# RMS norms on TensorE: row sums by four 128x32 column tiles, the spread by two tiles of 64 rows

## The chip, the cores and the metric

The kernel runs on one core of a Trainium2 chip. The metric is the device time of one launch, in microseconds. The kernel before takes 2510.49 us, the median of three runs (2510.39 to 2510.75). A core has five engines that work side by side, each through its own list of instructions in order: TensorE (PE, with its weight loads shown as PEld), VectorE (DVE), ScalarE (ACT), GpSimd (POOL) and SyncE (SP, which issues transfers). They wait for each other through semaphores.

## The reference

The reference is one inference step of a streaming encoder with two layers of width 1024, for 640 tokens (512 of a new stream, 8 x 16 of running ones). A layer is a half-step SwiGLU feed-forward block (inner width 2816), a mixer (short convolution and banded attention with 8 heads, gated and merged), and another half-step feed-forward block. Each starts with an RMS norm, and a last norm follows the second layer. All is float32.

```python
def _rmsnorm(x, g):
    xf = x.astype(jnp.float32)
    y = xf * lax.rsqrt(jnp.mean(xf * xf, axis=-1, keepdims=True) + EPS)
    return y.astype(x.dtype) * g

for l in range(DEPTH):
    x = x + 0.5 * _swiglu(_rmsnorm(x, norm_ffn1[l]), w_ffn1_gu[l], w_ffn1_down[l])
    m = _mixer(_rmsnorm(x, norm_mix[l]), ...)
    x = x + m
    x = x + 0.5 * _swiglu(_rmsnorm(x, norm_ffn2[l]), w_ffn2_gu[l], w_ffn2_down[l])
y = _rmsnorm(x, norm_final)
```

So there are seven norms: `a0`, the mixer's `m0`, `b0`, `a1`, `m1`, `b1`, and the final one.

## The kernel before

The state x lies transposed in the core's SBUF: eight tiles `x[k]` of 128 partitions (features) by 640 columns (tokens). Weights come as a stream of 128x1024 slabs (`raw`, issued by SP), are split by ACT and DVE into a high and a low part (`whi`, `wlo`, lines 320 and 325), and each product of float32 matrices is made of three matmuls in a fast format: high by high, high by low, low by high. Results gather in PSUM, whose tiles of one bank are named `att` or `pr`, and of two banks `acc`. Products that are computed by Strassen-like combinations of halves (line 410) write 128x320 at a time; the plain ones (line 387) write the two halves of 320 tokens in turn.

A norm's factor, one number a token, is applied after the product that needs it, so the product needn't wait for it. Its making has these steps:

1. ACT squares the eight tiles, DVE adds them into one 128x640 tile (`ssum`; in the mixer a part of `ya`).
2. `Stats.sums` (line 487): TensorE adds over the partitions. For each of five blocks of 128 tokens the block of `ssum` is the stationary operand and a column of ones the moving one, and the result, 128 tokens on 128 partitions, is one column of a PSUM tile (`nps`). Plain float32 is used here, for which the trace shows two records of weight load and matmul for each instruction.
3. `roots`, or `root` and `diagonal` (lines 599 and 603): ACT takes the square root of five columns, DVE the reciprocal.
4. `Stats.turn` (line 497): DVE multiplies the identity by each of the five columns: a 128x640 tile of five diagonals, written over `ssum`.
5. the spread (lines 609 and 469): TensorE multiplies a 128x128 tile of ones with the diagonals, in two matmuls of 320 tokens. It has each token's factor on all partitions (`nbc`), which ACT copies to SBUF (`rho` or `rr`).

The order of PE's instructions is written out by hand everywhere; in the feed-forward blocks' ends, in the mixer's second half and in the final norm the orders of DVE and ACT are too, while in the attention and between, a planner orders DVE's and ACT's steps. Products stand between steps 2 and 5 on PE, so that the root and the diagonal are made beside them: one part of a product of `gate_up` in a1, b0 and b1, more in a0 (`opening`) and in the mixers (line 1405, the values' product, with 128x512 at a time).

The final norm (`Final.all`) works on two parts of the tokens, 384 and 256. The last down product (line 1711) makes the first part for all eight `m`, then the second. The first part's sums (line 1680, six matmuls, for two tiles of squares) and spread (line 1740) stand within the second part's products. The second part's sums (line 1725) are added up piece by piece as the squares come; only the last piece, root, diagonal, spread and the eight outputs (line 1744, DVE, each followed by a transfer out) come after the last product.

For comparison, the sample attention uses column tiles of 32 already (lines 1546 and 1579: four heads' pairs beside each other, written to four ranges of 32 partitions), and the scores of the prompt attention use tiles of 64 rows (line 1452: two heads beside each other, written to two banks).

Of the kernel before, what the change touches and what calls it, by code (L numbers as in the profile page):

```python
# [10 lines left out]
F32 = mybir.dt.float32  # L11
F32R = mybir.dt.float32r
AF = mybir.ActivationFunctionType
ALU = mybir.AluOpType
PSUM = bass.MemoryType.PSUM

P = 128
D = 1024
L = 2
SEQ = 512  # L20
# [3 lines left out]
HT = T // 2  # L24
# [5 lines left out]
FF = 2816  # L30
KT = D // P
FT = FF // P
FH = FT // 2
CT = CW // P
CHUNK = 64
# [5 lines left out]
NP = KT // 2  # L41
NT = T // P

# [3 lines left out]

PARTS = slice(0, 3 * P), slice(3 * P, T)

# [14 lines left out]
O_G1, O_GM, O_G2, O_GF = 0, L * KT, 2 * L * KT, 3 * L * KT  # L64
# [44 lines left out]
def mixer_order():  # L109
# [74 lines left out]
def halves(t):  # L184
    return t.rearrange("p (a b) -> p a b", a=2)
# [3 lines left out]
def trunk(ctx: ExitStack, tc: tile.TileContext, xin, wst, small, pbias, samplebias, kcache, vcache,  # L189
          yout, ko, vo, co):  # L190
    nc = tc.nc
    PE, DVE, ACT, POOL, SP = nc.tensor, nc.vector, nc.scalar, nc.gpsimd, nc.sync

    cp = ctx.enter_context(tc.tile_pool(name="cp", bufs=1))
# [6 lines left out]
    ps = ExitStack()  # L201
# [31 lines left out]
    slabs, n = [], 0  # L233
# [10 lines left out]
    for kind, units in stages():  # L244
        n = sum(2 if z in ("gu", "mix") else 1 for z in units)
# [115 lines left out]
    class Tiles:  # L361


        def __init__(self):
            self.cur = None
            self.at = self.n = 0
# [47 lines left out]
    sm = cp.tile([P, NSM], F32, name="sm")  # L414
# [3 lines left out]
    ident = cp.tile([P, P], F32, name="ident")  # L418
    make_identity(nc, ident)
    ones = cp.tile([P, P], F32, name="ones")  # L420
    POOL.memset(ones, 1.0)
    epst = cp.tile([P, 1], F32, name="epst")
    POOL.memset(epst, EPS)
    early = cp.tile([P, 1], F32, name="early")
# [4 lines left out]
    x = [xp.tile([P, T], F32, name=f"x{k}") for k in range(KT)]  # L429
    for k in range(KT):  # L430
# [4 lines left out]
        if k % 2 == 0:  # L435
            c = slice(k * P, (k + 2) * P)
            SP.dma_start(raws[0][:, c], wst[0][:, c])

    def norm(name, goff, ssum, keep):

        out = []
        for k in range(KT):
            g = sm[:, goff + k : goff + k + 1]
            hi = hp.tile([P, T], F32R, tag="hhi", name=f"hhi{name}_{k}")
            lo = hp.tile([P, T], F32R, tag="hlo", name=f"hlo{name}_{k}")
            ACT.activation(hi, x[k], AF.Copy, scale=g)
            DVE.scalar_tensor_tensor(out=lo, in0=x[k], scalar=g, in1=hi.bitcast(F32),
                                     op0=ALU.mult, op1=ALU.subtract)
            out.append((hi, lo))
        for k in range(KT):  # L450
            if k == 0:
                ACT.activation(ssum, x[k], AF.Square)
            else:
                sq = tmp(f"sq{name}_{k}")
                ACT.activation(sq, x[k], AF.Square)
                DVE.tensor_tensor(out=ssum, in0=ssum, in1=sq, op=ALU.add)
        st = Stats(name)
        st.caps, st.rr = (keep.tile([P, T], F32, name=f"{n}{name}") for n in ("caps", "rr"))

        def sums():  # L460
            st.sums([ssum], st.bank)
            st.roots()
            st.turn(ssum, st.r)

        def spread():
            for a in range(2):
                c = slice(a * HT, (a + 1) * HT)
                ps = pr(f"nbc{name}_{a}")[:, :HT]
                PE.matmul(ps, ones, ssum[:, c], start=True, stop=True)
                ACT.copy(st.rr[:, c], ps)  # L470

        return out, st, (sums, spread)

    class Stats:


        def __init__(self, name):
            self.name = name
            self.s = sp.tile([P, NT], F32, tag="nrms", name=f"nrms{name}", bufs=3)
            self.r = sp.tile([P, NT], F32, tag="ninv", name=f"ninv{name}", bufs=2)  # L480

        def sums(self, parts, ps):

            self.ps = ps
            for c in range(NT):
                for i, z in enumerate(parts):
                    PE.matmul(ps[:, c : c + 1], z[:, c * P : (c + 1) * P], ones[:, 0:1],
                              start=i == 0, stop=i == len(parts) - 1)

        def roots(self):  # L490
            ACT.activation(self.s, self.ps[:, :NT], AF.Sqrt, bias=epst[:, 0:1], scale=1.0 / D)
            DVE.reciprocal(self.r, self.s)

        def turn(self, out, r):

            n = out.shape[1] // P
            DVE.tensor_tensor(out=out.rearrange("p (c t) -> p c t", c=n),
                              in0=ident.unsqueeze(1).to_broadcast([P, n, P]),
                              in1=r.unsqueeze(2).to_broadcast([P, n, P]), op=ALU.mult)

    def scaled(out, ps, rr):
        DVE.tensor_tensor(out=halves(out), in0=two(ps), in1=halves(rr), op=ALU.mult)
# [1 line left out]
    class Expand(Stats):  # L504
# [93 lines left out]
        def root(self):  # L598
            ACT.activation(self.s, self.ps[:, :NT], AF.Sqrt, bias=epst[:, 0:1], scale=1.0 / D)

# [3 lines left out]
            self.turn(self.ssum, self.r)  # L604

        def spread(self, ps):
            for a in range(2):
                c = slice(a * HT, (a + 1) * HT)
                PE.matmul(ps[a], ones, self.ssum[:, c], start=True, stop=True)
            for a in range(2):  # L610
                ACT.copy(self.rho[:, a * HT : (a + 1) * HT], ps[a])

            ACT.activation(early, epst, AF.Silu)
            self.known = True
# [1041 lines left out]
    class Final:  # L1656
# [7 lines left out]
        def all(self, ops):  # L1664
            ws = [[tiles.take() for _ in ops] for m in range(KT)]
            flush()
            rr = pool[0].tile([P, T], F32, tag="cap", name="frr", bufs=5)[:, PARTS[0]]
            A, B = PARTS

            for m in range(KT):  # L1670
                self.product(0, m, ops, ws[m])
                self.take(0, m, m < KT - 1)
            ends = self.ssum[0], self.sq
            for m in range(KT):
                self.product(1, m, ops, ws[m])
                if m == 1:
                    self.ps = att("npsf0")[:, : A.stop // P]
                    for b in range(A.stop // P):
                        for i, z in enumerate(ends):
                            PE.matmul(self.ps[:, b : b + 1], z[:, b * P : (b + 1) * P], ones[:, 0:1],  # L1680
                                      start=i == 0, stop=i == 1)
                    self.root(0)
                if m == 4:
                    ACT.copy(rr, self.spread(0))
                if m == 5:
                    self.ps = acc("npsf1")[:, :, 0]
                    self.add(self.ssum[1], True)
                if m > 4:
                    self.add(self.sq)
                self.take(1, m, m < 4)  # L1690
                if m == 2:
                    self.turn(0)
                for k in {5: (0,), 6: (1, 2)}.get(m, ()):
                    self.out(k, A, rr)
            self.add(self.sq, False, True)
            self.root(1)
            for k in range(3, 6):
                self.out(k, A, rr)
            self.turn(1)
            for k in range(6, KT):  # L1700
                self.out(k, A, rr)
            ps = self.spread(1)
            for k in range(KT):
                self.out(k, B, ps)

# [16 lines left out]
        def add(self, z, start=False, stop=False):  # L1722

            for b in range(2):
                PE.matmul(self.ps[:, b : b + 1], z[:, b * P : (b + 1) * P], ones[:, 0:1],
                          start=start, stop=stop)

        def root(self, a):
            cs = slice(PARTS[a].start // P, PARTS[a].stop // P)
            ACT.activation(self.st.s[:, cs], self.ps, AF.Sqrt,  # L1730
                           bias=epst[:, 0:1], scale=1.0 / D)

# [2 lines left out]
            DVE.reciprocal(self.st.r[:, cs], self.st.s[:, cs])  # L1735
            self.st.turn(self.ssum[a], self.st.r[:, cs])

        def spread(self, a):
            ps = att(f"nbcf{a}")[:, : PARTS[a].stop - PARTS[a].start]
            PE.matmul(ps, ones, self.ssum[a], start=True, stop=True)  # L1740
            return ps

        def out(self, k, c, rr):
            DVE.scalar_tensor_tensor(out=x[k][:, c], in0=x[k][:, c], scalar=sm[:, O_GF + k : O_GF + k + 1],
                                     in1=rr, op0=ALU.mult, op1=ALU.mult)
            (ACT if c == PARTS[1] and k % 2 else SP).dma_start(yout[:, k, c], x[k][:, c])

# [93 lines left out]
def _layout(inputs):  # L1841
    i = {n: np.asarray(a) for n, a in inputs.items()}
    tok = np.concatenate([i["x_prompt"].reshape(SEQ, D), i["x_sample"].reshape(NB * TS, D)])
    xin = tok.T.reshape(KT, P, T).transpose(1, 0, 2)
# [61 lines left out]
```

## Time and profile before

| | |
|---|---|
| median of three runs | 2510.49 us |
| span of the profiled execution, first to last instruction | 2509.0 us |
| mean granted TensorE clock | 0.999 |
| PE busy | 2492.6 us, 99% |
| DVE busy | 2127.7 us, 85% |
| ACT busy | 1322.0 us, 53% |
| POOL busy | 254.0 us, 10% |
| HBM | 92 GB/s over the span |

The page gives the profiled execution's span and no other time of it. The span leaves out what lies ahead of the first instruction and behind the last. In the rows, "L487" is a line of the kernel, `npsa<-ones,ssuma` what is written and read (buffer numbers left out), `128*128` the tile of the PE array in use (rows by columns), `128x1` the moving operand, and "x10" the number of records that a row groups. Matmuls overlap, so a record lasts longer than its distance to the next.

### The profile page before, as it was taken

The numbers are of one execution on the slowest core, as the hardware profiler recorded it, in microseconds if no ns is written. First come the engines' busy times: TensorE is split into PE (matmuls) and PEld (weight loads), VectorE is DVE, ScalarE is ACT, GpSimd is POOL, SyncE is SP. The second block draws the span as 40 slices with busy tenths as digits, with TensorE's granted clock in tenths as the row PEclk, the third lists the DMA queues.
The fourth block names the chain that finished last, engine by engine and source line by source line (L and its number), as shares of the span: only waits on it lengthen the run. The fifth ranks groups of instructions, "written<-read, shape, count | busy, mean of one in ns | idle before, by whom it ended". The sixth has DMA issues, their size and how long they took to land.

```text
span 2509.0 us, 43304 instructions
## 1 busy us (share of the span) xinstructions
PE 2492.6 (99%) x17192; PEld 2442.1 (97%) x17192; DVE 2127.7 (85%) x3443; ACT 1322.0 (53%) x2068; POOL 254.0 (10%) x377
## 2 busy tenths in 40 slices
PE   9999999999999999999999999999999999999998
PEld 8999999889999999999999999998899999999998
DVE  7889998888777899998699999988786768899997
ACT  7445556664444545555455555556644455455553
POOL 0001112112000001100001111121210000011111
PEclk9999999999999999999999999999999999999999
DMA  4233445334222234443224443443442222244534
GB/s 145 76 100 103 122 116 127 108 121 156 76 88 93 73 102 116 109 107 100 84 74 111 110 120 104 115 118 117 140 137 85 76 94 76 87 114 109 119 102 102
DMA packets 101003, 265.43 MB, mean 106 GB/s; under 512 B 11360, under 2 KB 46816, under 8 KB 100800
## 3 DMA queue, kind: packets, MB, share of 16 engines
q1 hardware_dynamic: 69408, 220.76, 27.8%
q0 software_dynamic: 30528, 41.26, 9.2%
q8 instruction: 135, 2.21, 0.4%
q10 hardware_dynamic: 864, 0.65, 0.1%
q14 instruction: 68, 0.56, 0.1%
HBM read 222.70 MB, written 7.94 MB: 92 GB/s over the span
## 4 chain that ended last, share of the span: by engine, by line
PE 96%; DVE 2%; issue 1%; ACT 1%; DMA 1%; SPq 0%; DVEq 0%; ACTq 0%; POOLq 0%
PE pab L410 12%; PE paa L410 11%; PE pcb L410 6%; PE pca L410 6%; PE daa L964 5%; PE py L387 4%; PE po L387 4%; PE qa L410 4%; PE dab L964 4%; PE pdb L387 4%; PE pbb L410 3%; PE pba L410 3%; PE dca L964 3%; PE ma_cv L410 2%; PE ma_qk L410 2%; PE pda L387 2%
## 5 line engine op out<-in xcount | busy, mean ns | idle before, releaser
L320 ACT CAST whi<-raw 128x1024 fp32r<-128x1024 f32 (+1 forms) x566 | 509.5, 904 | 392.9 <-PE pba L410 37.2
L325 DVE TENSOR_TENSOR wlo<-raw,whi 128x1024 fp32r<-128x1024 f32 (+1 forms) x566 | 585.6, 1037 | 139.1 <-ACT whi L320 136.8
L320 ACT CAST whi<-s 128x1024 fp32r<-128x1024 f32 (+1 forms) x152 | 144.4, 950 | 266.6 <-issue 91.6
L410 PE MATMUL pab<-xhib,whi 128*128 128x320 f32 x704 | 218.3, 310 | 0.3
L410 PE MATMUL pab<-xlob,whi 128*128 128x320 f32 x704 | 217.4, 309 | 0.0
L410 PE MATMUL pab<-xhib,wlo 128*128 128x320 f32 x704 | 217.4, 309 | 0.0
L410 PE MATMUL paa<-xhia,whi 128*128 128x320 f32 x640 | 198.1, 309 | 1.0 <-ACT c_a L845 0.7
L410 PE MATMUL paa<-xhia,wlo 128*128 128x320 f32 x640 | 197.5, 309 | 0.0
L410 PE MATMUL paa<-xloa,whi 128*128 128x320 f32 x640 | 197.5, 309 | 0.0
L325 DVE TENSOR_TENSOR wlo<-s,whi 128x1024 fp32r<-128x1024 f32 (+1 forms) x152 | 166.1, 1093 | 5.5 <-ACT whi L320 5.5
L986 POOL DMA_DIRECT2D x<-c_b x56 | 49.3, 1023 | 1067.1 <-DVE x L991 783.6
L986 POOL DMA_DIRECT2D x<-c_a x72 | 63.5, 1024 | 834.0 <-ACT whi L320 510.6
L410 PEld LDWEIGHTS pab<-xhib,whi 128*128 128x128 f32 x704 | 132.2, 188 | 0.9 <-ACT c_b L845 0.8
L410 PEld LDWEIGHTS pab<-xlob,whi 128*128 128x128 f32 x704 | 132.2, 188 | 0.2
L410 PEld LDWEIGHTS pab<-xhib,wlo 128*128 128x128 f32 x704 | 132.2, 188 | 0.0
L410 PEld LDWEIGHTS paa<-xhia,whi 128*128 128x128 f32 x640 | 120.1, 188 | 1.6 <-ACT c_a L845 0.9
L410 PEld LDWEIGHTS paa<-xloa,whi 128*128 128x128 f32 x640 | 120.1, 188 | 0.1
L410 PEld LDWEIGHTS paa<-xhia,wlo 128*128 128x128 f32 x640 | 120.1, 188 | 0.0
L410 PE MATMUL pcb<-xhib,wlo 128*128 128x320 f32 x352 | 108.9, 309 | 0.0
L410 PE MATMUL pcb<-xhib,whi 128*128 128x320 f32 x352 | 108.7, 309 | 0.0
L410 PE MATMUL pcb<-xlob,whi 128*128 128x320 f32 x352 | 108.7, 309 | 0.0
L264 DVE TENSOR_TENSOR raw<-raw,raw 128x512 f32<-128x512 f32 x152 | 103.8, 683 | 0.5
(683 smaller groups left out, 7992.8 us busy)
## 6 DMA issues: line engine op xcount, KB each, us to landing
raw<-in_wst SPq DMA_DIRECT2D x378, 512.0 KB, 3.6
x<-c_a POOLq DMA_DIRECT2D x72, 160.0 KB, 4.5
x<-c_b POOLq DMA_DIRECT2D x56, 160.0 KB, 3.4
kc<-in_kcache SPq DMA_DIRECT2D x32, 256.0 KB, 3.6
vc<-in_vcache SPq DMA_DIRECT2D x16, 512.0 KB, 4.6
x<-u_a POOLq DMA_DIRECT2D x36, 160.0 KB, 4.3
x<-u_b POOLq DMA_DIRECT2D x28, 160.0 KB, 4.1
bias<-in_pbias POOLq DMA_DIRECT2D x16, 256.0 KB, 3.7
```

What stands on the lines that cost most here:

```text
L264: DVE.tensor_tensor(out=out, in0=a, in1=b, op=ALU.add)
L320: ACT.copy(hi[:, d], src[:, c])
L325: DVE.tensor_tensor(out=lo, in0=src, in1=hi.bitcast(F32), op=ALU.subtract)
L387: PE.matmul(ps[:, a, :HT], w, x[:, a * HT : (a + 1) * HT], start=first and j == 0, stop=last and j == 2)
L410: PE.matmul(ps, a, b, start=start and kp == 0 and j == 0, stop=stop and kp == NP - 1 and j == 2, skip_group_check=True)
L964: PE.matmul(ps[u], w, y, start=start and i == 0 and j == 0, stop=i == 1 and j == 2, skip_group_check=True)
L986: POOL.dma_start(x[ms[2 * u + r]][:, cols], z[:, u], accum_op=ALU.add)
```

## The change

The sums use tiles of 32 columns: for each block of 128 tokens, four matmuls, each with 32 tokens' columns of `ssum` as the stationary operand, write 32 partitions each of the same PSUM column. The four are in different column groups of the array. Five matmuls become twenty (two records each, as before).

The diagonal is folded: `fold` is 128x64, the left half of the identity plus the right half, made once on POOL between `ones` and `epst`. DVE's product is 128x64 a block, 128x320 in all instead of 128x640. Row p of it holds the factor of the token on partition p, in column p or p - 64.

The spread multiplies 64 rows of ones with 64 rows of the folded diagonals: the upper half gives one half of each block's tokens, the lower half the other, in two matmuls on two tiles of 64 rows, written to two banks. In the feed-forward and final norms (`halved`) the sums take their tokens so that the upper 64 partitions of every column belong to the first half of the tokens and the lower to the second; there the result comes out in two contiguous halves. In the mixer's norms the tokens stay in order, because the reciprocals also scale the values by token, and ACT's copies write 64 columns of each block.

In the final norm the first part's copy is two copies of 192 columns instead of one of 384, and the outputs of the second part read the factor from two banks. The order of PE's instructions is otherwise the same; in the mixer the planner places a few of DVE's and ACT's steps around the diagonal and the copies differently.

```diff
+HP = P // 2
...
+    fold = cp.tile([P, HP], F32, name="fold")
+    POOL.tensor_tensor(out=fold, in0=ident[:, :HP], in1=ident[:, HP:], op=ALU.add)
     epst = cp.tile([P, 1], F32, name="epst")
...
-        st = Stats(name)
+        st = Stats(name, False)
...
         def spread():
-            for a in range(2):
-                c = slice(a * HT, (a + 1) * HT)
-                ps = pr(f"nbc{name}_{a}")[:, :HT]
-                PE.matmul(ps, ones, ssum[:, c], start=True, stop=True)
-                ACT.copy(st.rr[:, c], ps)
+            st.spread([pr(f"nbc{name}_{a}")[:, :HT] for a in range(2)], ssum, st.rr)
...
             for c in range(NT):
-                for i, z in enumerate(parts):
-                    PE.matmul(ps[:, c : c + 1], z[:, c * P : (c + 1) * P], ones[:, 0:1],
-                              start=i == 0, stop=i == len(parts) - 1)
+                self.column(ps[:, c : c + 1], parts, c)
+
+        def column(self, out, parts, c, start=True, stop=True):
+
+            for i, z in enumerate(parts):
+                for o in range(0, P, 32):
+                    t = c * P + o
+                    if self.halved:
+                        t = o // HP * z.shape[1] // 2 + c * HP + o % HP
+                    PE.matmul(out[o : o + 32], z[:, t : t + 32], ones[:, 0:1],
+                              start=start and i == 0, stop=stop and i == len(parts) - 1)
...
             n = out.shape[1] // P
-            DVE.tensor_tensor(out=out.rearrange("p (c t) -> p c t", c=n),
-                              in0=ident.unsqueeze(1).to_broadcast([P, n, P]),
-                              in1=r.unsqueeze(2).to_broadcast([P, n, P]), op=ALU.mult)
+            DVE.tensor_tensor(out=out[:, : n * HP].rearrange("p (c t) -> p c t", c=n),
+                              in0=fold.unsqueeze(1).to_broadcast([P, n, HP]),
+                              in1=r.unsqueeze(2).to_broadcast([P, n, HP]), op=ALU.mult)
+
+        @staticmethod
+        def rows(ps, turned):
+
+            for i in range(2):
+                q = slice(i * HP, (i + 1) * HP)
+                PE.matmul(ps[i], ones[q], turned[q, : ps[i].shape[1]], start=True, stop=True)
+
+        def spread(self, ps, turned, out):
+
+            self.rows(ps, turned)
+            z = out.rearrange("p (i t) -> p i t" if self.halved else "p (c i t) -> p i c t", i=2,
+                              **({} if self.halved else {"t": HP}))
+            for i in range(2):
+                ACT.copy(z[:, i], ps[i] if self.halved else ps[i].rearrange("p (c t) -> p c t", t=HP))
...
         def spread(self, ps):
-            for a in range(2):
-                c = slice(a * HT, (a + 1) * HT)
-                PE.matmul(ps[a], ones, self.ssum[:, c], start=True, stop=True)
-            for a in range(2):
-                ACT.copy(self.rho[:, a * HT : (a + 1) * HT], ps[a])
+            super().spread(ps, self.ssum, self.rho)
...
                     for b in range(A.stop // P):
-                        for i, z in enumerate(ends):
-                            PE.matmul(self.ps[:, b : b + 1], z[:, b * P : (b + 1) * P], ones[:, 0:1],
-                                      start=i == 0, stop=i == 1)
+                        self.st.column(self.ps[:, b : b + 1], ends, b)
...
-                    ACT.copy(rr, self.spread(0))
+                    self.st.spread([att(f"nbcf0_{i}")[:, : A.stop // 2] for i in range(2)], self.ssum[0], rr)
...
-            ps = self.spread(1)
+            ps = acc("nbcf1")[:, :, : (B.stop - B.start) // 2]
+            self.st.rows([ps[:, i] for i in range(2)], self.ssum[1])
...
             for b in range(2):
-                PE.matmul(self.ps[:, b : b + 1], z[:, b * P : (b + 1) * P], ones[:, 0:1],
-                          start=start, stop=stop)
+                self.st.column(self.ps[:, b : b + 1], [z], b, start, stop)
...
-            DVE.scalar_tensor_tensor(out=x[k][:, c], in0=x[k][:, c], scalar=sm[:, O_GF + k : O_GF + k + 1],
+            z = x[k][:, c]
+            y = z if c == PARTS[0] else halves(z)
+            DVE.scalar_tensor_tensor(out=y, in0=y, scalar=sm[:, O_GF + k : O_GF + k + 1],
                                      in1=rr, op0=ALU.mult, op1=ALU.mult)
```

More of the change, by code (lines that the diff above doesn't have):

```diff
@@ L465, in spread, with __init__ @@
         def spread():
-            for a in range(2):
-                c = slice(a * HT, (a + 1) * HT)
-                ps = pr(f"nbc{name}_{a}")[:, :HT]
-                PE.matmul(ps, ones, ssum[:, c], start=True, stop=True)
-                ACT.copy(st.rr[:, c], ps)
+            st.spread([pr(f"nbc{name}_{a}")[:, :HT] for a in range(2)], ssum, st.rr)
         return out, st, (sums, spread)
     class Stats:
-        def __init__(self, name):
-            self.name = name
+        def __init__(self, name, halved=True):
+            self.name, self.halved = name, halved
             self.s = sp.tile([P, NT], F32, tag="nrms", name=f"nrms{name}", bufs=3)
@@ L1736, in turn @@
             self.st.turn(self.ssum[a], self.st.r[:, cs])
[L1738 to L1741, printed above, removed]
         def out(self, k, c, rr):
-            DVE.scalar_tensor_tensor(out=x[k][:, c], in0=x[k][:, c], scalar=sm[:, O_GF + k : O_GF + k + 1],
+            z = x[k][:, c]
+            y = z if c == PARTS[0] else halves(z)
+            DVE.scalar_tensor_tensor(out=y, in0=y, scalar=sm[:, O_GF + k : O_GF + k + 1],
                                      in1=rr, op0=ALU.mult, op1=ALU.mult)
```

## The prediction

> **What bounds the kernel now.** First the page's busy times and its chain of work, then the waits of PE.
>
> ```profile
> PE 2492.6 (99%) x17192; PEld 2442.1 (97%) x17192; DVE 2127.7 (85%) x3443; ACT 1322.0 (53%) x2068; POOL 254.0 (10%) x377
> PE 96%; DVE 2%; issue 1%; ACT 1%; DMA 1%; SPq 0%; DVEq 0%; ACTq 0%; POOLq 0%
> PE nbcf L1740 <- DVE fsum L497: 1.0, 1, 1.0
> PE paa L410 <- ACT c_a L845: 0.7, 1, 0.7
> ```
>
> PE is busy 99% of the span, and the chain that ends last runs on it for 96%. Its waits are few; only the first of those two stands at a norm, in the kernel's last microseconds. So a microsecond less in PE's own order of work is a microsecond less in the end, unless a wait grows in its place. I therefore cost each edit in time from one regular matmul to the next around it.
>
> One norm before, by the timeline of PE in the first layer:
>
> ```profile
> 26.05 0.46 PE L387 MATMUL poa<-hhia,wlo 128*128 128x320 f32 x2
> 26.34 1.17 PE L487 MATMUL npsa<-ones,ssuma 128*128 128x1 f32 x10
> ...
> 27.75 0.46 PE L387 MATMUL poa<-hloa,whi 128*128 128x320 f32 x2
> ...
> 31.86 1.24 PE L609 MATMUL nbca<-ssuma,ones 128*128 128x320 f32 x4
> ...
> 33.23 0.46 PE L387 MATMUL poa<-hloa,whi 128*128 128x320 f32 x2
> ```
>
> Columns are start, duration, then what, with the number of records merged. Regular matmuls are paired: 26.34 - 26.05 = 0.29 us a pair, 0.147 each. Between the sums' start and 27.75 lies one regular pair, so the five sums (two records each) take 27.75 - 26.34 - 0.29 = 1.12 us. Likewise the spread takes 33.23 - 31.86 - 0.29 = 1.08, four records of 0.27.
>
> **The sums.** Five matmuls become twenty of 32 columns: 40 records in ten rounds of four column tiles. Such tiles stand in the trace of the sample attention, with wide moving operands:
>
> ```profile
> 557.51 1.12 PE L1546 MATMUL spss<-kc,bd 128*32 128x272 f32 x16
> ...
> 565.01 0.31 PE L410 MATMUL ma_b<-hhim,wlo 128*128 128x320 f32 x1
> 565.25 0.67 PE L1546 MATMUL spss<-kc,bd 128*32 128x272 f32 x8
> 565.73 0.40 PE L1579 MATMUL spy<-vn,ss 128*32 128x128 f32 x8
> 565.95 0.62 PE L1579 MATMUL spy<-vc,ss 128*32 128x128 f32 x16
> ...
> 566.75 0.31 PE L410 MATMUL ma_b<-hlom,whi 128*128 128x320 f32 x1
> 565.25 0.16 PEld L1546 LDWEIGHTS spss<-kc,bd 128*32 128x32 f32 x8 [0.19 <-issue]
> 566.50 0.19 PEld L410 LDWEIGHTS ma_b<-hhim,whi 128*128 128x128 f32 x1 [0.20 <-issue]
> L1546 PEld LDWEIGHTS spss<-kc,bd x128: 106/109/110, 557.5 to 1855.7; 128*32 128x32 f32 x128
> L1546 PE MATMUL spss<-kc,bd x128: 392/393/417, 557.5 to 1856.0; 128*32 128x272 f32 x128
> L1579 PE MATMUL spy<-vc,ss x256: 272/273/273, 566.0 to 1875.4; 128*32 128x128 f32 x128
> ```
>
> The last three rows, from the tiles' own view, have the least, median and longest duration of one in ns. Four tiles do run beside each other: the eight vn records, two rounds of four, take 565.95 - 565.73 = 0.22 us, 0.11 a round. The eight loads last 0.11 each and 0.16 together, so they start within 0.05, some 7 ns apart. The x16 row's last start is 1.12 - 0.39 = 0.73 after its first; less 0.02 of stagger that is a first load and three rounds, 0.71, while 565.25 to 565.73 is the load and two rounds, 0.48. So a round of 272 columns is 0.23 and a 32-column load 0.02 to 0.03.
>
> Changing the tiling costs. Into tiles: 565.01 + 0.147 = 565.16, but the first load starts at 565.25 and none is hidden: 0.09 + 0.03 = 0.12. Out of them: the last spy starts at 565.95 + 0.62 - 0.27 = 566.30 and streams until 566.41, the next load starts at 566.50, and the next regular matmul effectively at 566.75 - 0.147 = 566.60: 0.20. Together 0.32 for each visit.
>
> The unknown is a round with one moving column, c. Upper row: 0.109, the round of 128 columns. Lower: 0.027, four issues of 7 ns, or one load. The nearest row is today's sums, which have one moving column too: 1.12 for ten records, 0.112 each. That is the load of 128 columns, 0.107 (four times the 0.027 of 32), and 5 ns; a quarter of the load and the 5 ns give c = 0.032, which I take. A norm's sums then cost 0.32 + 9 x 0.032 = 0.61; for c = 0.109, 1.30; for 0.027, 0.56.
>
> [...]
>
> The second-layer norm shows a wait as well:
>
> ```profile
> 1267.07 1.25 PE L487 MATMUL npsa<-ones,ssuma 128*128 128x1 f32 x10
> 1268.41 0.31 PE L410 MATMUL paa<-xloa,whi 128*128 128x320 f32 x1
> 1270.03 1.24 PE L609 MATMUL nbca<-ssuma,ones 128*128 128x320 f32 x4
> 1267.84 0.48 DVE L264 TENSOR_TENSOR ua<-pca,c_a 128x320 f32<-128x320 f32 x1
> 1268.65 0.19 DVE L603 RECIPROCAL ninva<-nrmsa 128x5 f32<-128x5 f32 x1 [0.33 <-ACT nrmsa L599]
> 1268.95 0.82 DVE L497 TENSOR_TENSOR ssuma<-ident,ninva 128x640 f32<-128x640 f32 x1
> ```
>
> Here the sums take 1268.41 - 0.147 - 1267.07 = 1.19: the squares' last addition delays them by 0.07, which the later load of the tiled sums hides. I count 1.19 for the three norms of this kind (a1, b0, b1) and 1.12 for a0 and, taken like it, the two mixers: 3 x 0.58 + 3 x 0.51 = 3.27 us saved.
>
> **The spread.** Two matmuls of 128 rows become two of 64 rows beside each other, two rounds for four records. The scores already run so:
>
> ```profile
> 473.57 0.31 PE L410 MATMUL ma_qk<-hhim,wlo 128*128 128x320 f32 x1
> 473.81 2.43 PE L1452 MATMUL pss<-k,q 64*128 64x512 f32 x16
> 474.35 0.19 PEld L1452 LDWEIGHTS pss<-k,q 64*128 64x128 f32 x2 [0.23 <-issue]
> 474.78 0.85 PEld L1452 LDWEIGHTS pss<-k,q 64*128 64x128 f32 x10 [0.24 <-issue]
> ```
>
> A round of 512 columns is 474.78 - 474.35 = 0.43 for both tiles, the price of one matmul record. The first load costs 474.35 - 473.81 - 0.43 = 0.11, after 473.81 - 473.57 - 0.147 = 0.09: 0.20 in. Out I take 0.20 again, from the column tiles. The spread is then 0.40 + 2 x 0.27 = 0.94 for 1.08: 0.14 saved, 0.84 in six norms; at worst 0 were the tiles to collide, at best 0.54 each without the changes of tiling.
>
> **Diagonal, copies, fold.** DVE's 0.82 becomes the 0.48 of the 128x320 row. Is the spread late then? The sums end some 0.6 earlier; the reciprocal starts at about 1268.3, when the addition of 1267.84 ends, the diagonal is done by 1269.1, and PE comes to the spread at 1270.03 - 0.58 = 1269.45. It isn't late, and ACT's copies (same number, same size) come earlier too. In the mixers they become strided and the planner moves a few of ACT's and DVE's steps around them; PE waits for none there, so I take 0, within ±0.1 each. POOL's new addition stands ahead of `epst`:
>
> ```profile
> 1.36 0.09 POOL L423 MEMSET epst<- 128x1 f32 x1
> 1.66 1.28 ACT L620 ACT_TABLE_LOAD   x1 [1.66 <-PEq L1878]
> ```
>
> ACT wants `epst` only after the table load, at 2.94; between 1.45 and 2.94 there is room for a 128x64 addition. Without that cover its few tenths would delay the first cast.
>
> **The final norm.**
>
> ```profile
> 2489.21 0.28 PE L1680 MATMUL npsf<-ones,fsum 128*128 128x1 f32 x2
> ...
> 2490.66 0.28 PE L1711 MATMUL pdf<-alob,whi 128*128 128x256 f32 x1
> 2493.65 0.28 PE L1711 MATMUL pdf<-ahib,wlo 128*128 128x256 f32 x1
> 2494.87 0.28 PE L1711 MATMUL pdf<-alob,whi 128*128 128x256 f32 x1
> 2495.82 0.50 PE L1725 MATMUL npsf<-ones,fsum 128*128 128x1 f32 x4
> 2496.83 0.28 PE L1711 MATMUL pdf<-alob,whi 128*128 128x256 f32 x1
> 2489.25 1.28 ACT L1730 ACT_TABLE_LOAD   x1
> 2501.62 0.43 DVE fsum L497
> ```
>
> Regular matmuls are 0.12 apart here. The first sums cost 2490.66 - 0.12 - 2489.21 = 1.33, and 0.32 + 11 x 0.032 = 0.67 after: 0.66. Their spread cost 2494.87 - 2493.65 - 0.24 = 0.98 with a short wait for the diagonal; tiled, 0.40 + 2 x 0.16 = 0.72. But the root comes after a table load that ends at 2490.53 whatever PE does, so the diagonal moves up by only some 0.3 and PE, 0.66 ahead, waits 0.25 again. Net for both 0.67. The two additions at 2495.82, eight records before and 32 after, cost 2496.83 - 0.12 - 2495.82 = 0.89; after, 0.32 + 7 x 0.032 = 0.54 and 0.1 of waiting for a square, because the copy of the spread ahead of it on ACT is now two: 0.25 saved. Two more additions, four records before and 16 after, go from 4 x 0.112 to 0.32 + 3 x 0.032: 0.03 each. The fifth stands under DVE's work. At the very end DVE is the chain; its last diagonal, 128x256 at 0.43 (the row of the chain of waits), loses 128 columns of the 320 between 0.82 and 0.48: 0.14. The eight outputs behind it read two banks instead of one and keep their size: 0. Sum 1.12.
>
> **Sum.** 3.27 + 0.84 + 1.12 = 5.2 us. The page gives the profiled span, 2509.0; the median of the runs is 2510.5, 1.5 above, for what lies around the span. I forecast 2505.3, 0.21% faster.
>
> **Rivals.** The sum holds 6 x 9 + 11 + 7 + 3 + 3 = 78 distances of length c.
> 1. *Load, then matmul, in turn within a tile*: c about 0.054, twice the load. The sum is 5.2 - 78 x 0.022 = 3.5: 2507.0. Against it: today's 0.112 is hardly more than its load.
> 2. *Rounds no shorter than seen*, 0.109, 27 ns a record: 5.2 - 78 x 0.077 = -0.8, 2511.3. [...]
> 3. *Slower*: the four tiles' loads and matmuls with one column don't overlap at all, c = 4 x 0.054 = 0.21: 5.2 - 78 x 0.18 = -8.8, 2519.3. It loses from c = 0.099 on, by 0.2% from 0.163. The loads 7 ns apart speak against it.
> 4. *Absorbed*: in a1, b0 and b1 DVE follows closely; if it doesn't move up with PE, the 3 x 0.72 gained there is lost at the next wait (the 0.7 us for `c_a` is such a place): 2507.5. Against it: DVE's work there itself waits for PE's sums and spread.
>
> **How the numbers follow.** Forecast 0.57, rival 1 0.16, rival 2 0.09, rival 3 0.05, rival 4 0.13. About 0.2%, 5.0 us, is what a measurement of this kernel can tell from no change, and the forecast lies on that line: within it c from 0.027 (2504.9) to 0.040 (2505.9) and the ±0.1 of six norms fall on both sides, 0.40 beyond and 0.17 within. So faster 0.40; same 0.17 + 0.16 + 0.09 + 0.13 = 0.55; slower 0.05. The range takes in the forecast and rivals 1 and 4: 2504.4 to 2508.0.
>
> **What would show it.** In the changed kernel's timeline, sums of x40 records some 0.4 to 0.6 us long instead of 1.17, the next regular matmul 0.6 after the start and not 1.12; spreads 0.94; no new row of PE waiting for `ssum` in the waits; the `c_a` wait not above 0.7. A sums row of 1.3 means rival 2. The forecast is wrong if c is above 0.04, if the changes of tiling cost more for one column than for 128, or if DVE's wait grows.

## The result, and the profile after

The changed kernel takes 2505.76 us (median of 14 runs, 2504.87 to 2506.73) against 2510.74 us for the kernel before on the same chip (14 runs): a ratio of 0.998, 95% interval 0.9973 to 0.9986. It is faster by 4.98 us; 2505.3 us was forecast. The profiled execution, the slowest of its runs, has a span of 2505.0 us against 2509.0.

The page of the changed kernel, its busy times, its chain of work and one of its DMA queues, and then its waits of PE:

```profile
PE 2487.9 (99%) x17472; PEld 2433.1 (97%) x17472; DVE 2123.9 (85%) x3443; ACT 1322.0 (53%) x2069; POOL 254.2 (10%) x378
PE 96%; DVE 2%; ACT 1%; DMA 1%; issue 0%; SPq 0%; DVEq 0%; ACTq 0%
q8 instruction: 137, 2.24, 0.4%
```
```profile
PE nbcf L513 <- DVE fsum L504: 1.4, 2, 1.2
PE qa L411 <- ACT capsm L1300: 0.7, 1, 0.7
PE paa L411 <- ACT c_a L863: 0.5, 1, 0.5
```

The bound has not moved: PE is busy for 4.7 us less and still carries the chain. PE waits longer for the final norm's diagonals (1.4 us for two of them, the last one 1.2 instead of 1.0), less for `c_a` (0.5 instead of 0.7), and there is a new wait at the gates of the first mixer, to which the repeat below comes back.

The first norm by PE's timeline (start, duration, what, records merged):

```profile
25.68 0.46 PE L388 MATMUL poa<-hhia,wlo 128*128 128x320 f32 x2
26.07 0.51 PE L494 MATMUL npsa<-ones,ssuma 128*32 128x1 f32 x40
26.51 0.56 PE L388 MATMUL poa<-hhia,whi 128*128 128x320 f32 x2
26.91 0.45 PE L388 MATMUL poa<-hloa,whi 128*128 128x320 f32 x2
...
30.71 0.46 PE L388 MATMUL poa<-hhia,wlo 128*128 128x320 f32 x2
31.10 0.81 PE L513 MATMUL nbca<-ssuma,ones 64*128 64x320 f32 x4
31.84 0.56 PE L388 MATMUL poa<-hhia,whi 128*128 128x320 f32 x2
32.24 0.45 PE L388 MATMUL poa<-hloa,whi 128*128 128x320 f32 x2
```

The pair at 25.68 holds PE until 25.97 (0.294 us a pair). The pair after the sums counts from the next one backwards, 26.91 - 0.29 = 26.62, because its own second matmul is late. The sums take 26.62 - 25.97 = 0.65 us (0.64 from the unrounded times) instead of 1.12. The spread takes 32.24 - 0.29 - (30.71 + 0.29) = 0.94 instead of 1.08.

To see where the gain arises, the table gives by how much the same regular matmul starts earlier than in the profile before, in us, at times of the kernel before. In the row of 2502 it is the first matmul of the last spread, and in the last row the end of the span. The columns e0 to e4 are experiments, told below.

| at, us | what lies just before | changed | e0 | e1 | e2 | e4 |
|---|---|---|---|---|---|---|
| 26 | the start | 0.36 | 0.04 | 0.19 | 0.33 | -0.73 |
| 35 | norm a0 | 1.00 | 0.67 | 0.66 | 0.49 | -0.11 |
| 460 | mixer norm m0 | 1.60 | 1.28 | 1.09 | 0.68 | 0.46 |
| 848 | gates, nothing changed | 0.35 | 1.26 | 1.08 | 0.68 | 0.44 |
| 865 | norm b0 | 1.32 | 2.23 | 1.59 | 1.01 | 1.43 |
| 1285 | norm a1 | 2.29 | 3.24 | 2.00 | 1.32 | 2.40 |
| 1700 | mixer norm m1 | 2.91 | 3.84 | 2.43 | 1.48 | 3.09 |
| 2105 | norm b1 | 3.89 | 4.83 | 3.20 | 1.81 | 4.08 |
| 2502 | final norm | 4.76 | 5.77 | 3.96 | 1.81 | 5.19 |
| end | output transfers | 4.05 | 4.65 | 3.52 | 1.82 | 5.20 |

Two things in it were not forecast. b0, a1 and b1 each gain 1.0 us, not 0.72. And behind the last norm 0.7 us (changed) and 1.1 us (e0) are lost again, with nothing left for PE to do. The experiments went after these two, beside the price of the tiles.

### The profile page after: what moved, and what is told of

It reads as the page before. It is cut to its first block, busy times and chain, and to the rows that moved or that the text cites. A ratio compares the mean times of both kernels' runs of the same rounds, so it can differ in the third digit from the quotient of the medians.

```text
span 2505.0 us, 43861 instructions
## 1 busy us (share of the span) xinstructions
PE 2487.9 (99%) x17472; PEld 2433.1 (97%) x17472; DVE 2123.9 (85%) x3443; ACT 1322.0 (53%) x2069; POOL 254.2 (10%) x378
## 4 chain that ended last, share of the span: by engine, by line
PE 96%; DVE 2%; ACT 1%; DMA 1%; issue 0%; SPq 0%; DVEq 0%; ACTq 0%
PE pab L411 12%; PE paa L411 11%; PE pcb L411 6%; PE pca L411 6%; PE daa L982 5%; PE py L388 4%; PE po L388 4%; PE qa L411 4%; PE dab L982 4%; PE pdb L388 4%; PE pbb L411 3%; PE pba L411 3%; PE dca L982 3%; PE ma_cv L411 2%; PE ma_qk L411 2%; PE pda L388 2%
```

## The experiments

**e0: the changed kernel once more.** No edit.

> The changed kernel itself once more, for a second profile. In the first one PE waits 0.7 us for ACT's copy to capsm in the first layer's gates, 0.9 us of the gain is lost there, and DVE ahead of it waits 1.3 us for a weight slab. If that is chance of one transfer, it is missing in this profile or the loss stands elsewhere, and the median stays within 2505.0 to 2506.7. If it belongs to the change (PE now reaches the gates ahead of the slab), the same wait of 0.6 to 0.9 us is there again.

2505.97 us (11 runs), ratio 0.9982 (0.9973 to 0.9991), against 2510.55 for the kernel before in the set of e0 to e3. Its profile has no row of PE waiting for `capsm`, and the 1.25 us that the changed kernel's profile lost between 460 and 848 us, 0.9 of it at that wait, is not lost. So it belongs to that execution and not to the change: DVE waited 1.3 us there for a weight slab that landed 5.1 us after its issue, where e0's took 3.5.

**e1: column-tile sums alone**, with the old diagonal and spread; **e2: the other half alone**, in the six inner norms.

```diff
 e1, from the kernel before
+                for o in range(0, P, 32):
+                    t = c * P + o
+                    PE.matmul(out[o : o + 32], z[:, t : t + 32], ones[:, 0:1], ...)
 e2, from the kernel before
-            DVE.tensor_tensor(out=out.rearrange(...), in0=ident...)
+            DVE.tensor_tensor(out=out[:, : NT * HP].rearrange(...), in0=fold...)
-                PE.matmul(ps[a], ones, self.ssum[:, c], start=True, stop=True)
+                PE.matmul(ps[i], ones[q], turned[q, : ps[i].shape[1]], start=True, stop=True)
```

> Column tiles for all sums, the final norm's too; full diagonals and 128-row spreads as before. Theory (a round is a 32-column load and 5 ns, 0.032 us; 0.32 us for the two changes of tiling): each of six sums costs 0.64 us for 1.12 to 1.19, the final norm gains 0.8; 3.1 + 0.8 below the kernel before, 2506.8. Rival, the gain comes from the spread and from the shorter chain through the diagonal: 2509.5 or above. Rival, absorbed in a1, b0 and b1: 2508.3.

> Folded diagonal and spreads by two tiles of 64 rows in the six inner norms; sums by 128 columns and the final norm as before. Theory: each spread 0.94 us for 1.08, 0.14 x 6 = 0.8 below the kernel before, 2509.9. Rival, tiles of 64 rows are worth the whole half, 0.5 each: 2507.6. Rival, the change of tiling eats all: 2510.7.

e1: 2507.45 us, ratio 0.9988 (0.9979 to 0.9996), 3.1 us less than before, between the theory and its second rival. e2: 2509.29 us, ratio 0.9995 (0.9986 to 1.0004), 1.3 us less (the theory had 0.8), which the interval does not tell from nothing. Taken right around the norms (a step of the table holds what happens between two norms as well), the sums alone bring 0.5 us in each of b0, a1 and b1, the other half alone 0.33, together 0.83, and both at once 1.0. In e1 the timeline shows why the sums alone fall short, at b0:

```profile
848.74 0.82 DVE L503 TENSOR_TENSOR ssumb<-ident,ninvb 128x640 f32<-128x640 f32 x1
849.62 1.34 PE L615 MATMUL nbcb<-ssumb,ones 128*128 128x320 f32 x4
```

The old diagonal ends at 849.56, and the spread starts right behind it: with faster sums the long diagonal is what PE comes to too early. From regular matmul to regular matmul the spread costs 1.22 us there instead of 1.08. The folded one, 0.49 us, is done in time. So the sums by themselves are worth more than 0.5, and more than was forecast. PE's timeline of the kernel before, at a1:

```profile
1266.81 0.31 PE L410 MATMUL pca<-xhia,wlo 128*128 128x320 f32 x1
1267.07 1.25 PE L487 MATMUL npsa<-ones,ssuma 128*128 128x1 f32 x10
1268.41 0.31 PE L410 MATMUL paa<-xloa,whi 128*128 128x320 f32 x1
```

The product ahead of the sums holds PE until 1266.96, so they cost 1268.41 - 0.147 - 1266.96 = 1.31 us; the prediction counted 1.19, from their own start. In the changed kernel the same count is 0.65, so the sums save 0.66 in these norms. The other surplus is a wait further on. PE's timeline of the kernel before and then of the changed one, where the next block begins:

```profile
861.01 0.42 ACT L845 COPY c_b<-pab 128x320 f32<-128x320 f32 x1
861.05 0.31 PE L410 MATMUL pcb<-xhib,wlo 128*128 128x320 f32 x1
861.48 0.41 PE L410 MATMUL pab<-xhib,whi 128*128 128x320 f32 x1
```
```profile
859.69 0.42 ACT L863 COPY c_b<-pab 128x320 f32<-128x320 f32 x1
859.91 0.31 PE L411 MATMUL pcb<-xhib,wlo 128*128 128x320 f32 x1
860.16 0.41 PE L411 MATMUL pab<-xhib,whi 128*128 128x320 f32 x1
```

Before, the matmul into `pab` starts 0.43 us after the one ahead of it, when ACT's copy out of `pab` ends (861.43). After, ACT's copy ends at 860.11, and the distance is 0.25. ACT gained more than PE here, 1.32 against 1.14, so the wait shrank by 0.18. For `c_a` in a1 it is the 0.7 and 0.5 of the waits. e2's waits and then e1's show that it comes from the second half of the change:

```profile
PE paa L411 <- ACT c_a L853: 0.5, 1, 0.5
```
```profile
PE paa L410 <- ACT c_a L851: 0.7, 1, 0.7
```

**e3: tiles of 64 columns**, two beside each other instead of four.

```diff
-                for o in range(0, P, 32):
+                for o in range(0, P, HP):
-                    PE.matmul(out[o : o + 32], z[:, t : t + 32], ones[:, 0:1],
+                    PE.matmul(out[o : o + HP], z[:, t : t + HP], ones[:, 0:1],
```

> The changed kernel with sums by two tiles of 64 columns instead of four of 32: the same ten rounds, 20 records of two beside each other. Theory (a round is the load of one tile and 5 ns): 0.053 + 0.005 = 0.058 a round, sums 0.32 + 0.03 + 9 x 0.058 = 0.87 us, 0.23 more in six norms and 0.026 x 24 in the final one: 2.0 above the changed kernel, 2507.8. Rival, rounds are bound by the issue of 7 ns a record: half the records, 0.014 to 0.016 a round, and 0.9 below the changed kernel, 2504.9.

2506.34 us, ratio 0.9983 (0.9974 to 0.9992). The total lies halfway between theory and rival; PE's timeline is the theory's:

```profile
25.75 0.46 PE L388 MATMUL poa<-hhia,wlo 128*128 128x320 f32 x2
26.14 0.75 PE L494 MATMUL npsa<-ones,ssuma 128*64 128x1 f32 x20
26.82 0.56 PE L388 MATMUL poa<-hhia,whi 128*128 128x320 f32 x2
27.21 0.45 PE L388 MATMUL poa<-hloa,whi 128*128 128x320 f32 x2
```

The sums take 27.21 - 0.29 - 26.04 = 0.87 us, 0.23 more than with 32 columns. Between rounds lie 0.0585 us here and 0.0316 in the changed kernel (single records of the trace): half the load of 128 columns and 5 ns, a quarter of it and 5 ns. At the last spread e3 is 4.25 us ahead of before, and at the end still 4.25: it loses nothing at the outputs, where e0 loses 1.1. Against e4, which loses nothing there either, it is slower by 1.5 us if each is taken from the kernel before in its own set (4.2 and 5.7 us), where the theory has 2.0.

**e4, e6 and e8: what is lost at the outputs.** DVE's last outputs in the kernel before and in the changed one, and then the landing of the output transfers, in the same order:

```profile
2503.02 3.22 DVE L1744 SCALAR_TENSOR_TENSOR x<-x,sm,nbcf 128x256 f32<-128x256 f32 x8
DMA to landing us min/median/max: 1.8/1.9/2.2
```
```profile
2498.26 3.22 DVE L1757 SCALAR_TENSOR_TENSOR x<-x,sm,nbcf 128x256 f32<-128x256 f32 x8
DMA to landing us min/median/max: 1.9/2.5/3.9
```

The span ends 2509.0 - 2506.24 = 2.8 us after the last output before and 2505.0 - 2501.48 = 3.5 after. The latest transfers are the second to the fourth, at 3.3 to 3.9 us. In the stretch from 2490 to 2502 us, cut into 40 slices, the DMA engines' share of busy time in the changed kernel reads:

```profile
DMA  0000000000049300069980000099999999999999
GB/s 0 0 0 0 0 0 0 0 0 0 0 179 369 108 0 0 0 230 382 338 318 15 0 10 10 26 338 364 374 364 384 348 379 364 370 323 355 338 355 338
```

The second and third outputs, issued at 2494.4 and 2494.9, move most of their bytes from 2495.1 to 2496.3, but land only at 2498.2 and 2498.7. Up to 2497.8 there is a hole of 0 to 26 GB/s, about what one of 16 engines moves when all move 340. Then the backlog runs at 323 to 384 GB/s without a pause. The last eight outputs are 128 KB each, one every 0.39 us, 335 GB/s: there is no slack in which to catch up. In front of the hole lies one packet of queue q8, by the DMA view of 2495 to 2496 us; and SP's issue of the next output takes 1.45 us (least, median and longest in ns):

```profile
q8 instruction: 1, 0.02, 9.5%
L1759 SPq DMA_DIRECT2D out_yout<-x x12: 332/385/1453, 2492.6 to 2501.1; - x12
```

The trace has this packet of 16,384 bytes at 2495.42, 1.5 us long. From 2496.5 to 2496.9 us nothing but it is under way, and up to 2497.8 only ten small packets follow, almost singly, as if they were what the outputs had left on the one engine that it had held; the trace does not name the engine. The counts fit one packet for every 256 of PE's instructions: 137 packets, all of 16,384 bytes, for the 34,944 records of PE and PEld, and 135 for the 34,384 before. The change adds two by its 560 more records there, and so moves where the last one falls. The kernel before has it at 2498.9, 0.9 us long.

To test it, instructions were put ahead of the first product, where PE idles (e4 32 products, 128 instructions; e6 four, on the kernel before).

```diff
+    pads = [0] * 32
...
+        while pads:
+            pads.pop()
+            PE.matmul(ps[:32, 0, :1], ones[:, :32], ones[:, :1], start=True, stop=True)
```

> The changed kernel with 32 products of one 32-column tile of ones by one column put ahead of the first product, where TensorE waits until 5.1 us for its first weights anyway; they need about 1 us there and change nothing that is computed. They shift TensorE's instruction stream by 128 instructions. In the four runs of the changed kernel and of the column sums alone, a 16 KB packet of the instruction queue lies at 2494.4 to 2496.1 us, between the first output transfers, with 40 to 44 TensorE instructions left; the second and third output then land 3.8 to 4.3 us after their issue instead of 1.9, and the end comes 3.1 to 3.9 us after VectorE's last output instead of 2.8. Theory: that packet holds the outputs up. Here it falls with some 172 instructions left, ahead of the first output (about 2489): all outputs land 1.8 to 2.2 us after their issue, the end comes 2.8 us after VectorE's last output, and the time is 2505.0 us (2505.9 less 0.8 to 1.2, 2504.6 to 2505.3). Rival: the outputs hold each other up, because the folded diagonal and the shorter spread bring them closer together: the packet's place is no matter, outputs of 3.8 us and more stay, and the time stays at 2505.9 us (2505.6 to 2506.2).

> The kernel before with 4 such products (16 TensorE instructions) ahead of its first product, so that the last packet of the instruction queue comes with 45 TensorE instructions left instead of 29: at about 2497.2 us instead of 2498.9, while the first output is on its way and the next are issued. Theory that this packet holds the outputs up: the second and third output land 3 us or more after their issue, the end moves from 2.8 to 3.1 to 3.9 us after VectorE's last output, and the time rises from 2510.5 by 0.3 to 1.0 us, to 2511.2. Rival (only closer outputs collide, or the kernel before recovers in its wider gaps): latencies of 1.9 to 2.2 us and the same time, 2510.5 us (2510.2 to 2510.8).

The profiles that showed a late second and third output by then were three: the changed kernel's, e0's and e1's. e4: 2505.07 us (11 runs), ratio 0.9977 (0.9968 to 0.9986) against 2510.73 in the set of e4 to e6. The packet lies at 2491.6, and all outputs land at the ordinary pace. The intervals of e4 and e0 overlap, so that 0.9 us between their medians is not settled by the times alone; the trace is plainer. DVE's last outputs, and the landing:

```profile
2497.84 3.22 DVE L1762 SCALAR_TENSOR_TENSOR x<-x,sm,nbcf 128x256 f32<-128x256 f32 x8
DMA to landing us min/median/max: 1.8/1.9/1.9
```

The end is 2503.8 - 2501.06 = 2.7 us behind. e6: 2510.82 us, ratio 1.0001 (0.9992 to 1.001). The packet lies at 2497.5, and the first output lands 4.2 us after its issue, but the tail is 2.8 us and the time is that of the kernel before:

```profile
DMA to landing us min/median/max: 1.8/1.9/4.2
```

So the packet holds outputs up in the kernel before as well. There it does no harm: it meets the first output, the next two are 0.7 us late, and from the seventh on, behind a pause for the diagonal, all land in 1.9 us again. The rival named the recovery and the time, though not the 4.2 us; the late second and third outputs and the 2511.2 us of the theory did not come.

e8 is the control, with 256 instructions ahead, one whole packet, so that the last one falls where it fell; e7 is its partner with 116. Both begin with 26 wide products, which were to test something else too.

```diff
-    pads = [0] * 32
+    pads = [0] * 16 + [1] * 26        (e8: [0] * 51 + [1] * 26)
...
+            if pads.pop():
+                PE.matmul(ps[:, 0, :P], dense, dense, start=True, stop=True)
+            else: ...
```

> The changed kernel with 26 bfloat16 products of a 128x128 square of ones and 16 of the small float32 ones ahead of the first product (116 TensorE instructions, so that the last fetch comes with 160 left and clear of the outputs). Nothing that is computed changes. In every trace so far the first products of 320 columns take 0.267 us each and go over to 0.147 us at 8.6 to 12.9 us, 3.3 to 7.3 us after the first of them; with the small products alone ahead it was the latest, 12.9. Theory: TensorE speeds up a few us after it began to be kept busy, and the wide products, from 1.2 us on without a gap, bring that forward to about 5 us, so that no product of the kernel is slow; by 27 us this is worth 0.4 to 1.1 us against the run with small products (its loss there was 0.2 us against the kernel before, where the two runs of the changed kernel had gained 0.5 and 0.9), and the time is 2504.3 us (2503.8 to 2504.7) with the last output's tail at 2.8 us. Rival: the first stage is set by what it waits for (transfers and VectorE's low halves), not by TensorE's pace, or the extra work delays it as much: 2505.1 us (2504.7 to 2505.6).

> As the run before in this set, but with 51 small products instead of 16, so that 256 TensorE instructions in all are put ahead: exactly one packet of the instruction queue, which brings the last fetch back to 44 instructions before the end. A control on the place of the fetch with the extra work kept. The 35 more products take 0.03 to 0.06 us each, 1.1 to 2 us, in which the first product may start up to 1.5 us later. Theory that the fetch between the outputs costs 0.7 to 1.2 us: outputs of 3.8 us and more come back, the end is 3.1 us or more after VectorE's last output instead of 2.8, and the time is 0.7 to 2 us above the run before, 2505.4 us. Rival (the 0.9 us that the 128 instructions brought came from something else than where the fetch falls): outputs at 1.8 to 2.2 us, tail 2.8 us, and what is lost is lost by 27 us at the start.

e7: 2504.65 us, ratio 0.9975 (0.9966 to 0.9985). e8: 2508.26 us, ratio 0.9989 (0.998 to 0.9998), against 2510.75. In e8 the packet is back at 2495.8 and so are the late outputs:

```profile
DMA to landing us min/median/max: 1.9/2.4/4.1
2498.67 3.22 DVE L1767 SCALAR_TENSOR_TENSOR x<-x,sm,nbcf 128x256 f32<-128x256 f32 x8
```

with a tail of 2505.7 - 2501.89 = 3.8 us. Moved away and moved back, the packet takes the tail with it. The other profiles agree. In the four with a long tail (the changed kernel 3.5 us, e0 3.9, e1 3.1, e8 3.8) the packet begins 1.0 to 1.1 us after the issue of the second output. In e2 and e6 it begins as long after the first output's, which lands 4.2 us after its issue; in the kernel before it begins when the first output has landed, and in e3, e4, e5 and e7 ahead of the first one's issue. In these seven the tail is 2.7 to 2.8 us. e8 is 3.6 us slower than e7, more than the expected 0.7 to 2: in the profiles, which differ by 2.8, the tail makes 1.0 and the later start 1.0. Of the remainder 0.4 is one wait of PE for DVE's `gb` at 2456.9 us and 0.2 lies between m1 and b1; why they differ is not explained.

What e7 was to test beside it did not come about. In PE's timeline of e7 the first products are slow until 8.7 us, although PE has been busy since 1.0:

```profile
0.99 2.96 PE L391 MATMUL poa<-dense 128*128 128x128 bf16 x26 [0.99 <-POOL dense L428]
3.88 1.87 PE L393 MATMUL poa<-ones 128*32 128x1 f32 x32
...
8.51 0.54 PE L396 MATMUL poa<-hhia,wlo 128*128 128x320 f32 x2
8.89 0.46 PE L396 MATMUL poa<-hhia,whi 128*128 128x320 f32 x2
```

e8 begins with the same wide products, but has more small ones behind them:

```profile
3.88 3.46 PE L393 MATMUL poa<-ones 128*32 128x1 f32 x102
7.27 0.73 PE L396 MATMUL poa<-hhia,whi 128*128 128x320 f32 x2
10.47 0.66 PE L396 MATMUL poa<-hhia,whi 128*128 128x320 f32 x2
10.96 0.45 PE L396 MATMUL poa<-hloa,whi 128*128 128x320 f32 x2
```

Its trace records the full granted clock from 4.08 us, 3.1 us after the first wide product, then 0.50 from 7.50 to 10.91, and the full clock again. So the wide products could bring the change forward, but it did not outlast the small ones behind them, and the kernel's first products, which come 1.6 us later than in e7, are slow until 10.9 us. In e7 the trace has no such early change: its record begins at 8.69 us.

The time of e7 is in the theory's range, but not by its mechanism: at 35 us the lead over before is 0.6, as e0 has it without any such products (0.7). Whether e4's -0.1 there is chance or comes from its small products is not told apart. e7 has the lowest median of all kernels run, 1.3 us below e0's, with intervals that overlap.

**e5: no column sums at all in the feed-forward norms.** The ones square spreads the sum of squares over all partitions in one step, and ACT makes the scale by logarithm and exponential.

```diff
+                PE.matmul(ps[a], ones, self.ssum[:, a * HT : (a + 1) * HT], start=True, stop=True)
+                ACT.activation(self.rho[:, a * HT : (a + 1) * HT], ps[a], AF.Ln, bias=epst[:, 0:1], scale=1.0 / D)
...
+            ACT.activation(self.rho, self.rho, AF.Exp, scale=-0.5)
```

> The changed kernel, but in the four feed-forward norms the column sums, the root, the folded diagonal and the spread are replaced by two products of the whole square of ones with the squares' sum (each 320 columns in float32: 0.54 us, so 1.08 us together on TensorE), whose result is the sum on every partition; ScalarE takes its logarithm and then the exponential of minus one half of it. The reference's result is still computed. On TensorE 0.64 for the sums and 0.94 for the spread become 1.08, which is 0.5 us less in each of four norms; the last instruction fetch falls 236 instructions before the end and so clear of the outputs. Theory: ScalarE has slack enough for the longer chain of logarithm and exponential, and TensorE's saving counts whole: 2.0 us below the changed kernel without its late fetch, 2503.0 us (2502.5 to 2503.6). Rival: the two functions need one more table load of 1.3 us on ScalarE in each norm, the scale comes that much later than TensorE needs it, and each norm loses 0.5 us or more: 2505.0 us or above.

2510.11 us, ratio 0.9999 (0.999 to 1.0007), 5.0 us above e4: the rival, and by more than it said. ACT's timeline of e5 at b0, and a row of PE's waits that the changed kernel does not have:

```profile
847.40 1.28 ACT L632 ACT_TABLE_LOAD   x1
849.62 0.95 ACT L632 ACTIVATE rhob<-nbcb,epst 128x320 f32<-128x320 f32 x2 [0.94 <-PE nbcb L630]
850.46 1.05 ACT L321 CAST whi<-raw 128x1024 fp32r<-128x1024 f32 x1
851.53 1.28 ACT L635 ACT_TABLE_LOAD   x1
852.82 0.74 ACT L635 ACTIVATE rhob<-rhob 128x640 f32<-128x640 f32 x1
```
```profile
PE pab L411 <- DVE gb L265: 1.7, 3, 0.7
```

The scale is ready at 853.56, 5.3 us after PE began the products for it (848.27), two table loads and a cast on the way. DVE then frees PE's accumulators late, and PE waits: with the longer chain ACT and DVE end last here, and a shorter order on PE is worth nothing.

## Why the prediction was right

- *PE's order of work sets the end.* Right up to PE's last matmul: but for the one wait for `capsm`, the leads of the table stay with the kernel from norm to norm, within 0.3 us.
- *A round with one column, c = 0.032.* Measured 0.0316. The chosen neighbour, today's load of 128 columns, gave it: a quarter of that load and 5 ns; e3 shows the half. Rivals 1 to 3 (0.054, 0.109, 0.21) are excluded in the trace. Within a round the four tiles' records start 7 ns apart.
- *0.32 for each visit.* 0.64 - 9 x 0.032 = 0.35 measured: 0.03 more than estimated.
- *Sums 0.61, saving 0.51 in a0 and the mixers.* Measured 0.64 and 0.48 in a0; the mixers' sums save 0.43 each (e1).
- *Spread 0.94, saving 0.14.* This is what was measured; e2 gains 0.15 in a0 and in each mixer.
- *Sums of b0, a1 and b1 save 0.58, all in all 0.72 a norm; the diagonal is worth 0.* Here the size was off: 1.0 us a norm. Two terms make up the difference. The sums before cost 1.31 and not 1.19, because the 0.11 us between the last product and their start were left out, and they save 0.66. And the earlier ACT shortens the wait for `c_a` or `c_b` by 0.18, which the prediction had put at nothing among diagonal and copies. With the spread's 0.14 this makes 0.98. The folded diagonal costs nothing, as was said, but it is needed: the one of 0.82 us makes the spread 0.14 late, and 0.66 less 0.14 is the 0.5 of e1. Rival 4 had the sign of the wait wrong.
- *Final norm 1.12.* e4 gains 0.98 from 2488 to 2502, the last diagonal among it, and nothing more on the way to the end.
- *The eight outputs behind it: 0.* This is the step that failed. They keep their size on DVE, but the transfers behind them are not hidden: in the changed kernel 0.7 to 1.1 us go there, because of where an instruction packet falls. Without that (e4) the gain in the spans is 5.2, the sum that was forecast, but by another account: from 26 us on it gains 5.9, and 0.7 had been lost at the start.

The forecast of 2505.3 against 2505.76 thus rests on the right mechanism, with 0.8 us of gain not foreseen in three norms and 0.7 to 1.1 us of loss not foreseen at the outputs. That the two nearly cancel is luck. The range held. The 4.98 us lie a hair short of the 5.0 us that the prediction took for the line between the same and faster, to which it had given 0.55 and 0.40.

## What to carry to other kernels

Here a float32 matmul with one moving column cost its stationary load (0.112 us a record, of which the prediction's estimate gives 0.107 to the load of 128 columns), so splitting it into column tiles that load beside each other divided the cost (0.0316 us a round), less 0.35 us for each visit to the other tiling, in and out: ten records, 1.12 us in a0, came to 0.64. Shortening one step of a chain is worth its full amount only if the next step comes along, as the folded diagonal did here: without it the sums kept 0.5 of their 0.66 us. And after a change in the number of instructions, look at where the last instruction packets fall against transfers that the end waits for: here it cost 0.7 to 1.1 us.

## What the runs showed of the hardware

- One 16 KB instruction packet among output transfers delayed one (e2, e6) to four (e1) of them to 3.3 to 4.3 us from issue to landing, instead of 1.9. In the two kernels whose first output it met, the end came no later. Why the issue of the next output is longer as well (1.45 us in the changed kernel, where the median is 0.385), and all transfers pause (0 to 26 GB/s), was not tried.
- The first products of 320 columns take 0.267 us each and go over to 0.147 at 8.4 to 12.7 us, 3 to 7 us after the first one, differently in each execution. In each of the eleven traces this comes within 0.2 us of an entry of full granted clock (8.41 us in e5, 8.67 in the changed kernel, 12.66 in e4). Ahead of the first entry the views read 1.00 because nothing is on record there; e8's reads 0.50 while its products are slow. What this is worth is not shown by itself: by 26 us the traces lie up to 1.5 us apart (from 0.51 ahead of the kernel before in e6 to 1.01 behind it in e8), and the two latest changes, e8's and e4's, have the two greatest losses, but among the others the lead does not follow the change (0.33 in e2 with 10.2 us, -0.04 in e7 with 8.7). Counted from PE's first product, e7's change comes after 7.7 us and e8's first one after 3.1, with the same 26 wide products ahead; what sets the time is not shown.
